# A gate build on VectorE alone, with the dense stage's pools opened before the build: a two-layer hybrid network with product-key experts on one Trainium2 core

## Chip, cores and metric

One core of a Trainium2 chip runs the whole program in one launch. The metric is the device time of one execution in microseconds (us), lower is better.

## What is computed

Two layers over 512 latent and 256 context tokens of width 1024, in float32. Each layer is a normalisation, an input projection, three parallel groups of heads, an output projection, and then a feed-forward part of 16384 experts, of which each token uses 8 x 16. The change lies in this last part alone:

```
s = einsum('nhpd,hpkd->nhpk', (tok @ wq), sub_keys)      # 8 heads x 2 halves x 128 keys
idx, gate = top 16 of the 256 sums of the two top-16 lists, softmax     # per token and head
a = gelu(einsum('nd,nhkd->nhk', x, u_tab[idx])) * gate
out = einsum('nhk,nhkd->nd', a, v_tab[idx])
```

## The kernel before

The program is traced with Python loops that are fully unrolled. The framework puts the instructions of each engine into one fixed order, at compile time, by their place in the program (earlier goes first) and by when its own model of time thinks them ready; on the chip each engine, and the queue of DMA issues of SyncE (SP), runs its list strictly in that order and waits on semaphores. Tiles of a pool with the same tag share its buffers, and a pool that closes leaves its memory to the next one opened on the same side, once its tiles are released.

The expert part (`peer_lat`, L1268) does most latent tokens (512 in layer 0, 384 in layer 1) *densely*: instead of fetching experts, it multiplies all tokens with all 16384 experts in 128 blocks of 128, and a sparse matrix G [token, expert] of gates sets what counts. The rest (256 context tokens in layer 0, the last 128 latent tokens in layer 1) is *gathered*: generators (`gather`, L1208) fetch rows of `peer_uv` (u and v of one expert per partition, 8 KB each) with an indirect DMA issued on GpSimd (L1249) and use them with two VectorE instructions (L1231 dot product, L1223 accumulation). One step of a generator handles two such fetches. The order is:

1. `route` (L1050): scores, top 16, indices and gates.
2. `build_g` (L1308): G is made by products of one-hot matrices. An iteration handles 8 tokens: VectorE compares index halves with an iota (`goa` L1353, `gob` L1354), multiplies by the high half of the gate (`o1`, L1355) and the low half (`o2`, L1359; the trace calls both `go`), 16 small float16 matmuls (128x128) multiply them, ScalarE scales two PSUM banks into `gst` (L1365), and after four iterations SP stores 2 MB to `Gd` in DRAM (L199). 64 iterations in layer 0, 48 in layer 1. Of the `o2`, every third is on VectorE, the others on GpSimd.
3. `dense` (L1396): for each block c: load and split u into high and low float32r parts (`duh` L1377 on ScalarE, `dul` L1378), 24 matmuls for the hidden values (L1383) and a GELU (`dge` L1386); load and split v (L1450, L1451); multiply with G (`dcf`, then `dch`, `dcl`); 24 output matmuls of the block before (helper, L141). One load of G (`dG`, L1444) serves four blocks. Gather steps are spread over the 128 blocks (L1464).

To give TensorE something in route and build, the hidden values of some blocks are made *early* (`early`, L1389): 26 blocks (1, 6, ..., 126) in each layer, stored to DRAM, and loaded again in the dense stage (`Hd`). In them `dul` is computed on GpSimd. `advance` says where in the program a block stands: 8 after the route (L1288), one per five iterations of the build (L1357), the rest after the build (L1297). `steps(STEP_BUILD)` (L1358) puts 0.15 or 0.1 gather steps into each iteration.

Pools: `pe` (u and hidden of the early blocks, left side) closes before the dense stage; `pu`, `pg` (gathered rows, six buffers) open before the build; `gk`, `gw` belong to the build; `dw` holds all tiles of the dense stage and opens on the right side after the build has closed. PSUM changes hands at the same place (`pps.close()`, L1302): 2 banks `sm` for early blocks and 4 `mm` for the build before it, 6 or 7 `o` and 2 or 1 `h` after it.

Of the kernel before, what the change touches and what calls it, by code (L numbers as in the profile page):

```python
# [10 lines left out]
F32R = mybir.dt.float32r  # L11
# [5 lines left out]
OP = mybir.AluOpType  # L17
# [4 lines left out]
P = 128  # L22
D = 1024
# [20 lines left out]
SB = 4  # L44
TB = 32
UVB = 6
STEP_BUILD = (0.15, 0.1)
RH = 2
ROUTE = (0, 0)
TAIL = (8, 8)  # L50
EARLY = (tuple(range(1, 128, 5)), tuple(range(1, 128, 5)))
GSC = 32768.0
ADA_BUFS = 3
ADA_PROJ = 0.7
# [32 lines left out]
class Kern:  # L87
    def __init__(self, ctx, tc, a, dbg=None):
        self.ctx, self.tc, self.nc, self.a = ctx, tc, tc.nc, a
        self.dbg = dbg  # L90
        self.uid = 0
        self.ev = 0
        self.bg = []
        self.bg2, self.owed = None, 0.0
        self.todo = 0
        self.pace = 0.0
        self.clock = 0.0
        self.rate = 0.0
        self.gelu = False
        self.hold = False  # L100

    def pool(self, st, name, bufs=1, space=None, side=None):
        kw = {}
# [1164 lines left out]
    def peer_lat(self, l, jobs, xt, sx, pps):  # L1268
        nc, a = self.nc, self.a
        nd = DENSE[l]  # L1270
        last = SEQ // P - 1
        with ExitStack() as st:
            pk = self.pool(st, "pdk", side="right")
            xh, xl = x = tuple(self.T(pk, [P, KD, SEQ], F32R, tag="x" + t) for t in "hl")
            sr, se, spu = ExitStack(), ExitStack(), ExitStack()
            run(self.norm(l, 1, 0, x, xt, side="right"))
            sx.close()
            pr = self.pool(sr, "pdr", side="left")
            self.gelu = True
            if nd < SEQ:  # L1280
                with ExitStack() as s1:
                    xT = self.T(self.pool(s1, "xT", side="right"), [P, KD, P], tag="xT")
                    ts = slice(last * P, SEQ)
                    nc.vector.tensor_add(xT, xh[:, :, ts].bitcast(F32), xl[:, :, ts].bitcast(F32))
                    xn = self.token_major(pr, xT, 0)
            self.bg2 = self.early(l, self.pool(se, "pe", 2), xh, xl)
            r = self.route(l, 0, x, pr)
            self.advance(TAIL[l])  # L1288
            self.pu = self.pool(spu, "pu", 1, side="right")
            pg = self.pool(spu, "pg", 1, side="right")  # L1290
            self.bg = [self.gather(pg, l, 1, i, *job) for i, job in enumerate(jobs)]
            if nd < SEQ:
                self.bg.append(self.gather(pg, l, 0, last, xn, *r[last]))
            self.todo = len(self.bg) * (HK // 2 + 3)
            with ExitStack() as s1:
                self.build_g(s1, l, r)
            run(self.bg2 or ())  # L1297
            self.bg2 = None
            se.close()
            if nd == SEQ:  # L1300
                sr.close()
            pps.close()  # L1302
            with ExitStack() as s1:
                self.dense(s1, l, xh, xl)
            spu.close()
            sr.close()

    def build_g(self, st, l, r):  # L1308

        nc, a = self.nc, self.a  # L1310
        T = self.T
        nd = DENSE[l]
        pk = self.pool(st, "gk", side="right")
        pw = self.pool(st, "gw", 2, side="right")
        iota = T(pw, [P, P], tag="iotag")
        self.load(iota, a["iota"])
        iota4 = T(pk, [P, P, 4], F16, tag="iota4")
        nc.vector.tensor_copy(iota4, iota[:, :, None].to_broadcast([P, P, 4]))
        e16 = [T(pk, [P, nd], F16, tag=f"e16{j}") for j in range(4)]
        for i in range(-(-nd // P)):  # L1320
            idx, gate = r[i]
            ts = slice(i * P, min((i + 1) * P, nd))
            m = ts.stop - ts.start
            for j in range(3):
                if j == 2:
                    src = gate
                else:
                    ii = T(pw, [P, HK], I32, tag="gii")
                    if j == 0:
                        nc.vector.tensor_scalar(ii, idx, 7, 127, op0=OP.logical_shift_right, op1=OP.bitwise_and)  # L1330
                    else:
                        nc.vector.tensor_scalar(ii, idx, 127, None, op0=OP.bitwise_and)
                    src = T(pw, [P, HK], tag="gif")
                    nc.vector.tensor_copy(src, ii)
                pt = self.ps("tr")
                self.tr(pt[:, :P], src)
                if j < 2:
                    nc.scalar.copy(e16[j][:, ts], pt[:, :m])
                else:

                    sg = T(pw, [P, P], tag="gsg")
                    nc.scalar.activation(sg[:, :m], pt[:, :m], AF.Copy, scale=GSC)
                    nc.scalar.copy(e16[2][:, ts], sg[:, :m])
                    nc.vector.tensor_sub(e16[3][:, ts], sg[:, :m], e16[2][:, ts])
        n = 0
        for tb in range(nd // TB):
            stage = T(pw, [P, P, TB], tag="gst")
            for q in range(TB // 8):
                c0 = tb * TB + q * 8
                bc = lambda e: e[:, c0:c0 + 8].rearrange("p (g t) -> p g t", t=4)[:, :, None, :].to_broadcast([P, 2, P, 4])  # L1350
                it = iota4[:, None].to_broadcast([P, 2, P, 4])
                oa, ob, o1, o2 = (T(pw, [P, 2, P, 4], F16, tag=f"go{x}") for x in "ab12")
                nc.vector.tensor_tensor(oa, bc(e16[0]), it, op=OP.is_equal)  # L1353
                nc.vector.tensor_tensor(ob, bc(e16[1]), it, op=OP.is_equal)  # L1354
                nc.vector.tensor_tensor(o1, oa, bc(e16[2]), op=OP.mult)  # L1355
                n += 1
                self.advance(0.2)  # L1357
                self.steps(STEP_BUILD[l])  # L1358
                (nc.vector if n % 3 == 0 else nc.gpsimd).tensor_tensor(o2, oa, bc(e16[3]), op=OP.mult)  # L1359
                for g in range(2):  # L1360
                    gp = self.ps("mm")
                    for t in range(4):
                        for j, o in enumerate((o1, o2)):
                            self.mm(gp[:, t * P:(t + 1) * P], ob[:, g, :, t], o[:, g, :, t], j == 0, j == 1)
                    nc.scalar.activation(stage[:, :, q * 8 + g * 4:q * 8 + g * 4 + 4].rearrange("p i t -> p t i"),  # L1365
                                         gp.rearrange("p (t i) -> p t i", i=P), AF.Copy, scale=1.0 / GSC)
            self.load(self.Gd[l][:, :, tb, :].rearrange("s j x -> j s x"),
                      stage.rearrange("p (s i) t -> p s (i t)", i=SB))
# [20 lines left out]
    def early(self, l, pool, xh, xl):  # L1389

        for c in EARLY[l]:
            ge = self.hidden(l, c, pool, pool, xh, xl, "sm", self.nc.gpsimd)
            self.load(self.Hd[l, c], ge)
            yield

    def dense(self, st, l, xh, xl):  # L1396
        nc, a = self.nc, self.a
        T = self.T
        nd = DENSE[l]
# [40 lines left out]

        todo, done = self.todo - DEFER[l], 0
        for sb in range(NC // SB):
            G = T(pw, [P, nd // TB, SB, TB], tag="dG")
            self.load(G.rearrange("p b i t -> p b (i t)"), self.Gd[l][sb])  # L1444
            for ci in range(SB):
                c = sb * SB + ci
                v = T(pw, [P, D], tag="dv")
                self.load(v, a["peer_v"][l, c * P:(c + 1) * P, :])
                vh, vl = (T(pw, [P, D], F32R, tag="dv" + x, bufs=2 + rest) for x in "hl")
                nc.scalar.copy(vh, v)  # L1450
                nc.vector.tensor_sub(vl, v, vh.bitcast(F32))  # L1451
                if c in EARLY[l]:
                    ge = T(pw, [P, nd], tag="dge")
                    self.load(ge, self.Hd[l, c])
                else:
                    ge = self.hidden(l, c, pw, pw, xh, xl, "h", nc.vector)
                cf = T(pw, [P, nd], tag="dcf", bufs=1)
                nc.vector.tensor_mul(cf.rearrange("p (b t) -> p b t", t=TB), ge.rearrange("p (b t) -> p b t", t=TB),
                                     G[:, :, ci, :])
# [7 lines left out]
                if prev is not None:  # L1467
                    add(*prev)
                prev = (c, ch, cl, vh, vl)
        gB = T(pw, [P, D], tag="du")  # L1470
        self.load(gB, self.grow[l][1][0:1, :].to_broadcast([P, D]))
        xs = [T(pw, [P, D], tag=t) for t in ("dG", "dv", "dv", "dG")[:NT + rest]]
        for t, x in enumerate(xs):
            self.load(x, self.xsrc(l, 1, 0, t))
        add(*prev)
# [3 lines left out]
        for t, x in enumerate(xs):  # L1479
            for hf in range(2):  # L1480
                hs = slice(hf * 512, (hf + 1) * 512)
                tmp = T(pw, [P, 512], tag="duh")
                nc.vector.tensor_mul(tmp, o[t][hf] if t < NT else o4[:, hf], gB[:, hs])
                nc.vector.tensor_add(x[:, hs], x[:, hs], tmp)
            nc.gpsimd.dma_start(self.xdst(l, 1, 0, t), x)
# [172 lines left out]
```

## Time and profile before

| | |
|---|---|
| time, median of 3 runs (range) | 4478.73 us (4469.4 to 4480.89) |
| the profiled execution: time, span | 4476.18 us, 4474.4 us |
| mean granted TensorE clock | 0.94 |
| busy: TensorE matmul, VectorE, GpSimd, ScalarE | 89%, 73%, 38%, 35% |
| layer 0: build, gap, dense stage | 1012 to 1294 us, to 1317.5 us, to 2607 us |
| layer 1: build, gap, dense stage | 3286 to 3483.6 us, to 3500 us, to the end |

Rows of groups give the line, the engine, the operation, output <- inputs, shapes and xcount, then the busy time, the mean time of one in ns, and the idle time of the engine before them with what ended it. PE is TensorE, PEld its weight loads, DVE VectorE, ACT ScalarE, POOL GpSimd. Matmul ends are modelled: a matmul's own duration overlaps the next one's, so a sum of durations is not time; the busy time of many is.

### The profile page before, as it was taken

To read this page: it belongs to the slowest core of one execution; us is meant where nothing else is said; L and a number is where in the kernel's file an instruction comes from. 1 tells how busy PE (TensorE), PEld (TensorE's weight loads), DVE (VectorE), ACT (ScalarE), POOL (GpSimd) and SP (SyncE) were. 2 spreads that over 40 slices of the span, in tenths; PEclk is the share of its full clock that TensorE was granted. 3 is DMA by queue.
4 is the path that set the end of the run, shared out by engine and by line. 5 is a ranking of instruction groups with operands and counts; after the bars stand their busy time and mean duration, and the time that the engine had idled before them with its cause. 6 is when DMAs were issued, how large, how long until landed. Compare 5 with 4: busy or idle time off the path is not lost. (4 is left out here: it accounts for less than half of the span.)

```text
span 4474.4 us, 57073 instructions
## 1 busy us (share of the span) xinstructions
PE 3992.0 (89%) x20829; PEld 3352.4 (75%) x20829; DVE 3283.9 (73%) x6347; ACT 1571.2 (35%) x2562; POOL 1705.1 (38%) x1363
## 2 busy tenths in 40 slices
PE   7889878877869999999999969888868899999998
PEld 4568657666658888777888859677667799999998
DVE  2444686589978888788888755674889577777775
ACT  2332243325543333223323233433246333333332
POOL 2133354785633333233333133345876222222220
PEclk8899889988879999999999989989978899999999
DMA  7663221317779889888889634123257788788875
GB/s 264 226 208 108 60 71 62 112 61 221 227 250 352 332 333 335 322 319 324 338 334 343 247 114 119 50 81 100 65 164 216 265 307 303 294 311 301 301 300 168
DMA packets 429346, 996.46 MB, mean 223 GB/s; under 512 B 31448, under 2 KB 264280, under 8 KB 375816
## 3 DMA queue, kind: packets, MB, share of 16 engines
q1 hardware_dynamic: 372760, 586.46, 38.3%
q0 software_dynamic: 56304, 406.35, 24.4%
q8 instruction: 164, 2.69, 0.2%
q14 instruction: 118, 0.97, 0.1%
HBM read 909.97 MB, written 81.17 MB: 222 GB/s over the span
## 5 line engine op out<-in xcount | busy, mean ns | idle before, releaser
L1249 POOL DMA_INDIRECT uv<-in_peer_uv_dram,ridx x384 | 633.3, 1649 | 1558.2 <-DVE eacc L1223 1506.8
L141 PE MATMUL o<-dvh,dch 128*128 128x512 f32 x1792 | 702.0, 392 | 3.5 <-DVE do L1425 3.5
L141 PE MATMUL o<-dvl,dch 128*128 128x512 f32 x1792 | 701.3, 391 | 0.0
L141 PE MATMUL o<-dvh,dcl 128*128 128x512 f32 x1792 | 697.2, 389 | 0.0
L1383 PE MATMUL h<-xh,duh 128*128 128x512 f32 (+1 forms) x1632 | 602.9, 369 | 47.5 <-ACT duh L1377 39.9
L1383 PE MATMUL h<-xh,dul 128*128 128x512 f32 (+1 forms) x1632 | 604.8, 371 | 0.4 <-DVE dul L1378 0.3
L1383 PE MATMUL h<-xl,duh 128*128 128x512 f32 (+1 forms) x1632 | 602.2, 369 | 0.0
L1223 DVE SCALAR_TENSOR_TENSOR eacc<-uv,egf,eacc 128x1024 f32<-128x1024 f32 x381 | 492.4, 1293 | 0.0
L1231 DVE SCALAR_TENSOR_TENSOR uv<-uv,xn 128x1024 f32<-128x1024 f32 x384 | 470.3, 1225 | 0.0
L1377 ACT CAST duh<-du 128x1024 fp32r<-128x1024 f32 x256 | 268.7, 1050 | 535.4 <-PE h L1383 455.6
L1378 DVE TENSOR_TENSOR dul<-du,duh 128x1024 fp32r<-128x1024 f32 x204 | 249.5, 1224 | 261.9 <-ACT duh L1377 225.6
L141 PEld LDWEIGHTS o<-dvh,dch 128*128 128x128 f32 x1792 | 336.3, 188 | 78.1 <-DVE do L1425 7.2
L141 PEld LDWEIGHTS o<-dvh,dcl 128*128 128x128 f32 x1792 | 336.5, 188 | 73.6 <-DVE dcl L1462 0.3
L141 PEld LDWEIGHTS o<-dvl,dch 128*128 128x128 f32 x1792 | 336.3, 188 | 66.6
L1450 ACT CAST dvh<-dv 128x1024 fp32r<-128x1024 f32 x256 | 263.1, 1051 | 350.1 <-PE o L141 298.0
L1451 DVE TENSOR_TENSOR dvl<-dv,dvh 128x1024 fp32r<-128x1024 f32 x256 | 308.8, 1221 | 101.5 <-ACT dvh L1450 82.1
L1383 PEld LDWEIGHTS h<-xh,duh 128*128 128x128 f32 x1632 | 309.1, 189 | 90.2 <-ACT duh L1377 40.5
L1383 PEld LDWEIGHTS h<-xl,duh 128*128 128x128 f32 x1632 | 309.0, 189 | 42.1
L1383 PEld LDWEIGHTS h<-xh,dul 128*128 128x128 f32 x1632 | 308.6, 189 | 39.1 <-DVE dul L1378 1.9
L141 PE MATMUL mm<-go,gob 128*128 128x128 f16 x1792 | 238.1, 297 | 94.0 <-DVE go L1355 79.0
L141 PEld LDWEIGHTS <-gob 128*128 128x128 f16 x1792 | 194.8, 120 | 141.4 <-DVE go L1355 100.6
L1365 ACT ACTIVATE gst<-mm 128x512 f32<-128x512 f32 x224 | 226.3, 1120 | 166.3 <-PE mm L141 153.6
(352 smaller groups left out, 8027.9 us busy)
## 6 DMA issues: line engine op xcount, KB each, us to landing
du<-in_peer_ut_dram SPq DMA_DIRECT2D x256, 512.0 KB
dv<-in_peer_v_dram SPq DMA_DIRECT2D x256, 512.0 KB
Gd<-gst SPq DMA_DIRECT2D x28, 2048.0 KB
wa<-in_w_ada_dram SPq DMA_DIRECT2D x24, 2048.0 KB
w<-in_w_in_dram SPq DMA_DIRECT2D x78, 512.0 KB
dG<-Gd SPq DMA_DIRECT2D x32, 1024.0 KB
w<-in_peer_wq_dram SPq DMA_DIRECT2D x48, 512.0 KB
dG<-Gd SPq DMA_DIRECT2D x32, 768.0 KB
```

Source lines behind the costliest of these rows:

```text
L141: self.nc.tensor.matmul(out, lhsT=lhsT, rhs=rhs, start=start, stop=stop)
L1223: nc.vector.scalar_tensor_tensor(acc, t[:, D:], w, acc, op0=OP.mult, op1=OP.add)
L1231: nc.vector.scalar_tensor_tensor(t[:, :D], t[:, :D], 1.0, xn, op0=OP.mult, op1=OP.mult, accum_out=dots[:, k:k + 1])
L1249: nc.gpsimd.indirect_dma_start(t, None, a["peer_uv"], bass.IndirectOffsetOnAxis(ap=idx[:, k:k + 1], axis=0))
L1365: nc.scalar.activation(stage[:, :, q * 8 + g * 4:q * 8 + g * 4 + 4].rearrange("p i t -> p t i"), gp.rearrange("p (t i) -> p t i", i=P), AF ...
L1377: nc.scalar.copy(uh, u)
L1378: eng.tensor_sub(ul, u, uh.bitcast(F32))
L1383: nc.tensor.matmul(hp[:, :nd], lhsT=lt[:, k], rhs=rt[:, k, :nd], start=n == 0, stop=n == 3 * KD - 1)
L1450: nc.scalar.copy(vh, v)
L1451: nc.vector.tensor_sub(vl, v, vh.bitcast(F32))
```

## The change

`o2` is always on VectorE; no gather step stands in the build; the early blocks that are emitted inside the build loop take `dul` on VectorE (those ahead of and behind the loop stay on GpSimd); 25 blocks are early (3, 8, ..., 123). `pe` stays open through the dense stage, whose u and hidden tiles come from it. A new pool `pv` for v, its halves and G opens before the build, `pu` and `pg` after it. In block 0 the load of G is emitted behind the load of u. The tiles of the final addition come from other tags.

```
-STEP_BUILD = (0.15, 0.1)
-EARLY = (tuple(range(1, 128, 5)), tuple(range(1, 128, 5)))
+EARLY = (tuple(range(3, 128, 5)), tuple(range(3, 128, 5)))
...
-            self.bg2 = self.early(l, self.pool(se, "pe", 2), xh, xl)
+            pe = self.pool(se, "pe", 2)
+            self.bg2 = self.early(l, pe, xh, xl)
             r = self.route(l, 0, x, pr)
             self.advance(TAIL[l])
+            pv = self.pool(spu, "pv", 2, side="right")
+            self.building = True
+            with ExitStack() as s1:
+                self.build_g(s1, l, r)
+            self.building = False
+            run(self.bg2 or ())
+            self.bg2 = None
             self.pu = self.pool(spu, "pu", 1, side="right")
...
-            with ExitStack() as s1:
-                self.build_g(s1, l, r)
-            run(self.bg2 or ())
-            self.bg2 = None
-            se.close()
-            if nd == SEQ:
-                sr.close()
             pps.close()
             with ExitStack() as s1:
-                self.dense(s1, l, xh, xl)
+                self.dense(s1, l, xh, xl, pe, pv)
             spu.close()
+            se.close()
             sr.close()
...
+                nc.vector.tensor_tensor(o2, oa, bc(e16[3]), op=OP.mult)
                 self.advance(0.2)
-                self.steps(STEP_BUILD[l])
-                (nc.vector if n % 3 == 0 else nc.gpsimd).tensor_tensor(o2, oa, bc(e16[3]), op=OP.mult)
...
-            ge = self.hidden(l, c, pool, pool, xh, xl, "sm", self.nc.gpsimd)
+            ge = self.hidden(l, c, pool, pool, xh, xl, "sm", self.nc.vector if self.building else self.nc.gpsimd)
...
-            G = T(pw, [P, nd // TB, SB, TB], tag="dG")
-            self.load(G.rearrange("p b i t -> p b (i t)"), self.Gd[l][sb])
+            G = T(pv, [P, nd // TB, SB, TB], tag="dG")
+            if sb:
+                self.load(G.rearrange("p b i t -> p b (i t)"), self.Gd[l][sb])
...
-                    ge = self.hidden(l, c, pw, pw, xh, xl, "h", nc.vector)
+                    ge = self.hidden(l, c, pe, pe, xh, xl, "h", nc.vector)
+                if c == 0:
+                    self.load(G.rearrange("p b i t -> p b (i t)"), self.Gd[l][0])
...
-        gB = T(pw, [P, D], tag="du")
+        gB = T(pv, [P, D], tag="dv")
...
-        xs = [T(pw, [P, D], tag=t) for t in ("dG", "dv", "dv", "dG")[:NT + rest]]
+        xs = [T(p, [P, D], tag=t) for p, t in ((pv, "dG"), (pv, "dG"), (pv, "dv"), (pe, "du"))[:NT + rest]]
...
-                tmp = T(pw, [P, 512], tag="duh")
+                tmp = T(pe, [P, 512], tag="dge")
```

In `dense` the tiles `dv`, `dvh`, `dvl` move from `pw` to `pv` and the early blocks' `dge` from `pw` to `pe` in the same way.

## Rows read from the trace of the kernel before

**Rows 1.** The page: busy time of the engines, and one group of instructions
```profile
PE 3992.0 (89%) x20829; PEld 3352.4 (75%) x20829; DVE 3283.9 (73%) x6347; ACT 1571.2 (35%) x2562; POOL 1705.1 (38%) x1363
...
L1378 DVE TENSOR_TENSOR dul<-du,duh 128x1024 fp32r<-128x1024 f32 x204 | 249.5, 1224 | 261.9 <-ACT duh L1377 225.6
```

**Rows 2.** Busy time by stretch: both builds, the gaps behind them, dense stages
```profile
core 0: us, PE busy (x) PEld busy (x) DVE busy (x) ACT busy (x) POOL busy (x), PEclk, DMA share, GB/s
...
1012.00:1294.00 282.00, 223.89 (x1387) 180.15 (x1385) 268.32 (x278) 151.69 (x178) 166.41 (x76) 0.87 0.70 223
1294.00:1317.50 23.50, 0.04 (x1) 0.04 (x1) 3.90 (x8) 3.33 (x5) 2.71 (x2) 0.50 0.87 301
1317.50:2400.00 1082.50, 1071.36 (x4602) 867.65 (x4603) 932.13 (x1255) 326.55 (x491) 351.17 (x212) 0.99 0.88 331
...
3286.00:3483.60 197.60, 157.77 (x1062) 139.20 (x1060) 187.22 (x185) 113.22 (x132) 121.07 (x53) 0.85 0.67 209
3483.60:3500.00 16.40, 0.01 (x1) 0.02 (x1) 1.07 (x1) 2.58 (x3) 0.00 (x0) 0.58 0.94 309
3500.00:4400.00 900.00, 899.65 (x4446) 811.66 (x4447) 668.10 (x885) 331.88 (x493) 197.89 (x118) 1.00 0.79 296
```

**Rows 3.** Groups of instructions in the build of layer 0
```profile
L141 PE MATMUL mm<-go,gob 128*128 128x128 f16 x1024 | 136.2, 297 | 55.4 <-DVE go L1355 48.4 <-POOL go L1359 5.5 <-DVE go L1359 0.4
...
L1359 POOL TENSOR_TENSOR go<-goa,e 128x1024 f16<-128x1024 f16 x43 | 99.5, 2318 | 85.8 <-DVE goa L1353 59.9 <-PE mm L141 21.9 <-DVE e L1344 2.9
L1355 DVE TENSOR_TENSOR go<-goa,e 128x1024 f16<-128x1024 f16 x64 | 98.2, 1534 | 0.0
L1353 DVE TENSOR_TENSOR goa<-e,iota 128x1024 f16<-128x1024 f16 x64 | 62.3, 981 | 0.1
...
L1378 POOL TENSOR_TENSOR dul<-du,duh 128x1024 fp32r<-128x1024 f32 x14 | 39.3, 2809 | 5.3 <-ACT duh L1377 3.6 <-issue 1.7
...
L1223 DVE SCALAR_TENSOR_TENSOR eacc<-uv,egf,eacc 128x1024 f32<-128x1024 f32 x14 | 22.7, 1625 | 0.0
L1231 DVE SCALAR_TENSOR_TENSOR uv<-uv,xn 128x1024 f32<-128x1024 f32 x17 | 20.5, 1212 | 0.0
L1359 DVE TENSOR_TENSOR go<-goa,e 128x1024 f16<-128x1024 f16 x21 | 14.3, 680 | 0.0
```

**Rows 4.** VectorE in order of time in the build of layer 0 (start, us)
```profile
1055.16 2.38 DVE L1355 TENSOR_TENSOR go<-goa,e 128x1024 f16<-128x1024 f16 x1
1057.46 0.68 DVE L1353 TENSOR_TENSOR goa<-e,iota 128x1024 f16<-128x1024 f16 x1
...
1059.87 0.68 DVE L1353 TENSOR_TENSOR goa<-e,iota 128x1024 f16<-128x1024 f16 x1
```

**Rows 5.** Matmuls of line 1383 alone, by stretch (busy, count; clock, DMA)
```profile
1012.00:1294.00 282.00, 110.81 (x355) 69.10 (x353) 0.87 0.70 223
...
3286.00:3483.60 197.60, 74.27 (x288) 55.45 (x287) 0.85 0.67 209
...
3500.00:4400.00 900.00, 425.75 (x2304) 411.93 (x2305) 1.00 0.79 296
```

**Rows 6.** SP's queue, then TensorE, at the end of layer 0's build
```profile
1295.06 0.37 SPq L199 DMA_DIRECT2D Gd<-gst  x1
1309.03 0.33 SPq L199 DMA_DIRECT2D dG<-Gd  x1
...
1309.88 0.42 SPq L199 DMA_DIRECT2D du<-in_peer_ut_dram  x1
...
1317.46 0.80 PE L1383 MATMUL h<-xh,duh 128*128 128x512 f32 x1 [23.53 <-ACT duh L1377]
```

**Rows 7.** SP's queue at the end of layer 1's build
```profile
3482.57 0.37 SPq L199 DMA_DIRECT2D Gd<-gst  x1
...
3491.41 0.32 SPq L199 DMA_DIRECT2D dG<-Gd  x1
```

**Rows 8.** Waits of SP's queue, layer 0's build: us, times, longest
```profile
SPq L199 <- ACT gst L1365: 130.6, 18, 12.4
```

More of the change, by code (lines that the diff above doesn't have):

```diff
@@ L1285, in peer_lat @@
                     xn = self.token_major(pr, xT, 0)
-            self.bg2 = self.early(l, self.pool(se, "pe", 2), xh, xl)
+            pe = self.pool(se, "pe", 2)
+            self.bg2 = self.early(l, pe, xh, xl)
             r = self.route(l, 0, x, pr)
             self.advance(TAIL[l])
+            pv = self.pool(spu, "pv", 2, side="right")
+            self.building = True
+            with ExitStack() as s1:
+                self.build_g(s1, l, r)
+            self.building = False
+            run(self.bg2 or ())
+            self.bg2 = None
             self.pu = self.pool(spu, "pu", 1, side="right")
@@ L1344, in build_g @@
                     nc.vector.tensor_sub(e16[3][:, ts], sg[:, :m], e16[2][:, ts])
-        n = 0
         for tb in range(nd // TB):
@@ L1355, in build_g @@
                 nc.vector.tensor_tensor(o1, oa, bc(e16[2]), op=OP.mult)
-                n += 1
+                nc.vector.tensor_tensor(o2, oa, bc(e16[3]), op=OP.mult)
                 self.advance(0.2)
-                self.steps(STEP_BUILD[l])
-                (nc.vector if n % 3 == 0 else nc.gpsimd).tensor_tensor(o2, oa, bc(e16[3]), op=OP.mult)
                 for g in range(2):
@@ L1391, in early, with dense @@
         for c in EARLY[l]:
-            ge = self.hidden(l, c, pool, pool, xh, xl, "sm", self.nc.gpsimd)
+            ge = self.hidden(l, c, pool, pool, xh, xl, "sm", self.nc.vector if self.building else self.nc.gpsimd)
             self.load(self.Hd[l, c], ge)
             yield
-    def dense(self, st, l, xh, xl):
+    def dense(self, st, l, xh, xl, pe, pv):
         nc, a = self.nc, self.a
@@ L1442, in dense @@
         for sb in range(NC // SB):
-            G = T(pw, [P, nd // TB, SB, TB], tag="dG")
-            self.load(G.rearrange("p b i t -> p b (i t)"), self.Gd[l][sb])
+            G = T(pv, [P, nd // TB, SB, TB], tag="dG")
+            if sb:
+                self.load(G.rearrange("p b i t -> p b (i t)"), self.Gd[l][sb])
             for ci in range(SB):
                 c = sb * SB + ci
-                v = T(pw, [P, D], tag="dv")
+                v = T(pv, [P, D], tag="dv")
                 self.load(v, a["peer_v"][l, c * P:(c + 1) * P, :])
-                vh, vl = (T(pw, [P, D], F32R, tag="dv" + x, bufs=2 + rest) for x in "hl")
+                vh, vl = (T(pv, [P, D], F32R, tag="dv" + x, bufs=2 + rest) for x in "hl")
                 nc.scalar.copy(vh, v)
@@ L1452, in dense @@
                 if c in EARLY[l]:
-                    ge = T(pw, [P, nd], tag="dge")
+                    ge = T(pe, [P, nd], tag="dge")
                     self.load(ge, self.Hd[l, c])
                 else:
-                    ge = self.hidden(l, c, pw, pw, xh, xl, "h", nc.vector)
+                    ge = self.hidden(l, c, pe, pe, xh, xl, "h", nc.vector)
+                if c == 0:
+                    self.load(G.rearrange("p b i t -> p b (i t)"), self.Gd[l][0])
                 cf = T(pw, [P, nd], tag="dcf", bufs=1)
```

## The prediction, made before the change was run

> **What bounds the kernel now.** The page comes first: TensorE's matmuls are busy 89% of the span, VectorE 73% [rows 1]. Such a share is a mean over stages, so the next view is the busy time by stretch [rows 2]. In the two dense stages TensorE is busy 1071.36 of 1082.5 us and 899.65 of 900, at clock 0.99 and 1.00: they can lose, but hardly win. In the two builds it is busy 223.89 of 282 and 157.77 of 197.6 us, at 0.87 and 0.85, while VectorE is busy 268.32 (95%) and 187.22 (95%). Behind each build stands a gap, 23.5 and 16.4 us, in which no compute engine works. What can be won lies in 282 + 23.5 + 197.6 + 16.4 = 519.5 us; the rest of the span is taken as it is.
>
> The groups of the build show why VectorE is full [rows 3]. In the idle time ahead of the build's matmuls 48.4 of 55.4 us end with `o1`. The same kind of product, same shapes, takes 680 ns as `o2` and on average 1534 as `o1`; `goa` takes 981. In order of time [rows 4] an `o1` has 2.38 us where a GpSimd product runs, and five instructions, 1057.46 to 1059.87, start 0.60 us apart where none does. VectorE and GpSimd hold each other up here: a product given to GpSimd (2318 ns) lengthens the one VectorE does meanwhile by about 1.7 us, more than the 0.6 it spares.
>
> **Part 1, `o2` on VectorE, no gather steps, early `dul` on VectorE.** An iteration costs VectorE four products at 0.60, 2.41 us by the starts in [rows 4]. Layer 0: 64 x 2.41 = 154, twelve `dul` in the loop (advance: 8 + 0.2 x 64) at 1.22 [rows 1] = 15, the five blocks behind the loop still on GpSimd at 1.7 of hindrance = 9, some 6 of set-up (an estimate): 184 us. Layer 1: 116 + ten `dul` 12 + seven blocks 12 = 140 and a few. The gather takes 20.5 + 22.7 = 43 us out of the first build [rows 3].
>
> TensorE then sets the pace. Layer 0: the 1024 small matmuls have 136.2 us [rows 3]; 355 hidden matmuls were in the build [rows 5], one block of 24 goes, and at 1071.36 / 4602 = 0.233 us [rows 2] 331 cost 77: 213 us. Layer 1: 768 at the same 0.133 = 102, plus 264 at 425.75 / 2304 = 0.185 [rows 5] = 49: 151. ScalarE (151.69 and 113.22 us busy) stays below. No build has run TensorE-bound, so the excess over this floor lies between 0 and 15% (it is 26% and 24% of TensorE's busy time now, with VectorE in the way; in a dense stage 1%). I take 5%, nearer the dense stage, because the lists are again fixed by a model that sees TensorE with slack: 224 and 159 us. **Gain 58 and 38.6 us** (37 to 69, 24 to 47).
>
> The Trainium skill, Perfetto Trace Analysis, "Optimizing Scalar/DVE Operations", says that offloading to GpSimd may make sense when VectorE is saturated, which speaks against taking work back at 95%, and adds that between these two it might not help, as they share a port. By its first half the builds would not get shorter (the third rival); [rows 4] are the measurement of its second half, and the sum goes by them.
>
> **Part 2, the pools opened ahead.** Now G's last store goes out at 1295.06, its load can go at 1309.03, and u and v stand behind it in SP's list although they don't need it; the first matmul starts at 1317.46 [rows 6]. In layer 1 store and load are 3482.57 and 3491.41 [rows 7]. With `pe` and `pv` open, v and u of blocks 0 and 1 can be there before the build ends, and u of block 2 as soon as a buffer is free; blocks 0 to 2 are not early, so TensorE has three hidden blocks that need no G: 3 x 24 x 0.233 = 16.8 us, and 13.3 in layer 1. Of the gaps 6.7 and 3.1 us stay, and some 2 us in layer 1 until the PSUM banks change hands: I take 6 and 5. **Gain 17.5 and 11.4 us**; bounds nothing and the whole gap. Late next is G itself: its wait now stands behind one u and v, and the loads queued behind it (v, u of later blocks) wait for it in SP's list. `pu` opens in memory that the build gives up, so six row fetches of 1 MiB start just then, on DMA engines that were 0.87 busy in the gap; that is inside the bounds.
>
> **Part 3, small ones.** One block less is early: its 24 matmuls, counted out of the builds above, are in the dense stages, 5.6 and 4.4 us **lost**, and its `dul` now costs VectorE there; one store and load of its hidden values less, at nothing. The moved gather steps (some 9 and 4) add 43 us to a VectorE that is idle 1082.5 - 932 = 150 us in the stretch of layer 0's dense stage shown, beside a bound TensorE: hidden, but its DMA rises from 0.88 to about 0.92 busy (20 MB more on some 425). I take 4 us **lost**, from 0 to 12; without the cover all 43 would show. The tiles of the last addition come from other tags with the same number of buffers and their loads stand behind two free slots: nothing, or one load (the 8.4 us from 1309.03 to 1317.46, [rows 6]) if a slot is late. `pe` and the route's results held longer: the next layer starts from the dense stage's output anyway, nothing.
>
> **Sum**: 58 + 38.6 + 17.5 + 11.4 - 5.6 - 4.4 - 4 = 111.5 us. The profiled execution took 4476.2, so 4364.7; the median of the runs is 2.5 above it: **4367 us**.
>
> **Rivals.**
> *The gaps stay.* If v and u of block 1 stay behind G's wait in SP's list, or PSUM passes on late, hardly more than nothing of the 28.9 us is won: 82.6 gained, 4396. For it: SP's list has had that order. Against it: the buffers now exist before the build ends. 0.18.
> *TensorE's list is poor.* With 15% over the floor (245 and 174), bare gaps and 12 us lost in the dense stages, 37 + 24 - 10 - 12 = 39 to 60 us are gained: about 4427. For it: lists fixed by a model; 0.13.
> *VectorE is not relieved* (the change doesn't do what it says, and what the skill's first half would give): durations stay, and VectorE takes over 43 + 32 products at 0.68 and 22 `dul` at 1.22, less the gathers: 268 - 43 + 29 + 15 = 269 in layer 0 (nothing won) and 187 + 22 + 12 - 21 = 200, 13 more, in layer 1. With the gaps and part 3 the sum is +2: 4477. Against it: [rows 4]. 0.06.
> *VectorE stands behind `dul`* (slower). On GpSimd a subtraction that waited for its u held up little; on VectorE all products of the build are queued behind it, and TensorE behind those. SP waits up to 12.4 us for a `gst` [rows 8], with u queued behind it. If each of the 22 `dul` waited that long: 273 us, 162 more than all gains, 4640. It decides from a wait of about (111 + 40 of VectorE's slack) / 22 = 7 us each. Against it: before, 14 of them waited 3.6 us together for `duh` [rows 3]. 0.05.
>
> **Numbers.** The forecast has 0.58. With the best bounds (69 + 47 + 40 - 10 = 146) the time is 4333; the poor list ends at 4440. The range 4330 to 4425 leaves out the slower rival, the third one and part of the second. A measurement of this kernel can tell 0.3%, 13 us, from no change. Faster: 0.58 + 0.18 + 0.13 = 0.89; same 0.06; slower 0.05.
>
> **What would show it.** Right: `o1` and `goa` near 680 ns on average; builds of about 224 and 159 us with TensorE above 90% busy, clock near 1; hidden matmuls within a few us of the last small one, before G lands; dense stages within some 10 us. Wrong: `o1` still above 1 us; VectorE idle in the build behind `duh`; gaps above 15 us; a dense stage with DMA at 0.95 or more and TensorE waiting for u.

## The result, and the profile after

The changed kernel takes 4374.32 us (median of 4 runs, 4370.12 to 4378.36) against 4479.81 for the kernel before on the same chip: a ratio of 0.9768, 95% interval 0.9747 to 0.9788. The prediction was 4367. The profiled execution has a span of 4368.4 us, 106.0 less than before.

The page of the kernel after: busy time by engine, then groups [rows 1, 3].

```profile
PE 3969.8 (91%) x20829; PEld 3338.2 (76%) x20829; DVE 3179.7 (73%) x6446; ACT 1570.0 (36%) x2562; POOL 1467.7 (34%) x1264
...
L1377 DVE TENSOR_TENSOR dul<-du,duh 128x1024 fp32r<-128x1024 f32 x228 | 278.6, 1222 | 303.3 <-ACT duh L1376 287.5
...
L141 PE MATMUL mm<-go,gob 128*128 128x128 f16 x1792 | 232.9, 296 | 8.7 <-DVE go L1357 5.8
```

The last line holds the first part of the result: over both builds the small matmuls now wait 8.7 us, where layer 0's alone waited 55.4. (Lines behind L1346 moved up by one.) The groups of layer 0's build say why [rows 3]:

```profile
L141 PE MATMUL mm<-go,gob 128*128 128x128 f16 x1015 | 133.8, 296 | 4.6 <-DVE go L1357 4.2 <-ACT gst L1364 0.2
...
L1356 DVE TENSOR_TENSOR go<-goa,e 128x1024 f16<-128x1024 f16 x64 | 43.8, 684 | 0.0
L1357 DVE TENSOR_TENSOR go<-goa,e 128x1024 f16<-128x1024 f16 x64 | 43.7, 683 | 0.0
L1354 DVE TENSOR_TENSOR goa<-e,iota 128x1024 f16<-128x1024 f16 x64 | 43.3, 684 | 0.0
```

`o1` (L1356) takes 684 ns instead of 1534, `goa` 684 instead of 981: within 4 ns of what `o2` took on VectorE before (680). All 64 `o2` have come to VectorE, and VectorE is busy 173 us where it was 268.

Busy time by stretch: layer 0's build, what follows it up to the first dense hidden matmul, its dense stage, then the same of layer 1 [rows 2].

```profile
1002.10:1197.00 194.90, 190.26 (x1287) 159.41 (x1286) 173.24 (x277) 148.20 (x165) 4.91 (x2) 0.94 0.74 212
1197.00:1231.30 34.30, 25.28 (x117) 20.79 (x115) 3.79 (x3) 10.71 (x13) 13.10 (x9) 0.93 0.96 344
1231.30:2400.00 1168.70, 1166.59 (x5030) 945.71 (x5031) 1050.40 (x1427) 354.87 (x543) 410.15 (x246) 1.00 0.91 349
...
3185.60:3339.00 153.40, 139.71 (x1004) 128.60 (x1003) 129.05 (x207) 111.27 (x127) 11.24 (x2) 0.90 0.70 205
3339.00:3387.60 48.60, 33.81 (x162) 31.33 (x160) 1.60 (x2) 11.93 (x16) 19.68 (x12) 0.82 0.85 308
3387.60:4300.00 912.40, 912.37 (x4501) 813.88 (x4502) 682.91 (x907) 333.82 (x499) 204.21 (x122) 1.00 0.79 298
```

Both builds became much shorter (282 to 194.9 us, 197.6 to 153.4). But what lies behind them grew, from 23.5 to 34.3 and from 16.4 to 48.6 us, and its nature changed: TensorE now works there. What it works on is in the same view of the hidden matmuls alone (L1382; a block is 24 of them). The stretches are route, build, and what follows, of each layer:

```profile
770.00:1002.10 232.10, 63.43 (x232) 47.37 (x232) 0.85 0.26 81
1002.10:1197.00 194.90, 72.98 (x264) 48.23 (x262) 0.94 0.74 212
1197.00:1231.30 34.30, 24.28 (x106) 19.85 (x106) 0.93 0.96 344
2800.00:3185.60 385.60, 46.87 (x211) 41.92 (x211) 0.86 0.23 73
3185.60:3339.00 153.40, 49.66 (x231) 42.20 (x230) 0.90 0.70 205
3339.00:3387.60 48.60, 33.81 (x162) 31.33 (x160) 0.82 0.85 308
```

In layer 0, 232 matmuls (9.7 blocks) ran ahead of the build, 264 in it, and 106 (over four blocks) are left behind it; in layer 1 8.8, 9.6 and 6.8 blocks. These left-over *early* blocks, not blocks 0 to 2 of the dense stage, now stand behind the builds, and TensorE idles 9 us after them in layer 0 and 15 us among them in layer 1. In the kernel before, 271 and 338 matmuls (11.3 and 14.1 blocks) ran ahead of the builds, by the same view of its two routes, and the rest, 355 and 288, in them [rows 5]:

```profile
780.00:1012.40 232.40, 74.61 (x271) 55.81 (x272) 0.89 0.28 86
...
2800.00:3286.70 486.70, 70.82 (x338) 65.09 (x338) 0.91 0.24 75
```

Cut at the first `goa`, the first dense hidden matmul and the last output matmul of each layer (before, that of layer 0 is at 2611.6 us, behind the 2607 of the table above), the 106.0 us are:

| stretch | before | after | difference |
|---|---|---|---|
| up to layer 0's build | 1012.4 | 1002.1 | -10.3 |
| layer 0, build and what follows | 305.1 | 229.2 | -75.9 |
| layer 0, dense stage | 1294.1 | 1287.5 | -6.6 |
| up to layer 1's build | 675.1 | 666.8 | -8.3 |
| layer 1, build and what follows | 213.3 | 202.0 | -11.3 |
| layer 1, dense stage to the end | 974.4 | 980.8 | +6.4 |

Layer 0 won what was forecast (-75.5). Layer 1 won 11 us where 50 were forecast, so the runs had two things to find: whether the products on VectorE are the cause of the shorter builds, and where layer 1's gain went.

### The profile page after: what moved, and what is told of

Same layout as the page of the kernel before. It is cut to its first block, busy times and chain, and to the rows that moved or that the text cites. A ratio compares the mean times of both kernels' runs of the same rounds, so it can differ in the third digit from the quotient of the medians.

```text
span 4368.4 us, 56981 instructions
## 1 busy us (share of the span) xinstructions
PE 3969.8 (91%) x20829; PEld 3338.2 (76%) x20829; DVE 3179.7 (73%) x6446; ACT 1570.0 (36%) x2562; POOL 1467.7 (34%) x1264
## 4 chain that ended last, share of the span: by engine, by line
PE 58%; DVE 5%; issue 3%; DMA 3%; POOL 3%; ACT 1%; SPq 0%; POOLq 0%; ACTq 0%; DVEq 0%
PE o L141 27%; PE h L1382 22%; PE mm L141 6%; PE sm L1382 2%; DMA du<-in_peer_ut_dram 2%; POOL roh L1174 1%; PE tr L196 0%; POOL dul L1377 0%; PE sm L141 0%; DMA w<-in_w_in_dram 0%; DVE req L1172 0%; POOL wl L321 0%; DVE go L1356 0%; DVE go L1357 0%; DVE gob L1355 0%
## 5 line engine op out<-in xcount | busy, mean ns | idle before, releaser
L141 PE MATMUL o<-dvl,dch 128*128 128x512 f32 x1792 | 711.1, 397 | 0.0
L141 PE MATMUL o<-dvh,dcl 128*128 128x512 f32 x1792 | 707.1, 395 | 0.0
L1382 PE MATMUL h<-xh,duh 128*128 128x512 f32 (+1 forms) x1648 | 600.5, 364 | 12.5 <-ACT dge L1385 12.5
L1382 PE MATMUL h<-xl,duh 128*128 128x512 f32 (+1 forms) x1648 | 599.8, 364 | 0.0
L1382 PE MATMUL h<-xh,dul 128*128 128x512 f32 (+1 forms) x1648 | 598.5, 363 | 0.0
L1377 DVE TENSOR_TENSOR dul<-du,duh 128x1024 fp32r<-128x1024 f32 x228 | 278.6, 1222 | 303.3 <-ACT duh L1376 287.5
L1382 PEld LDWEIGHTS h<-xh,duh 128*128 128x128 f32 x1648 | 309.9, 188 | 53.8 <-ACT dge L1385 14.1
L1382 PEld LDWEIGHTS h<-xl,duh 128*128 128x128 f32 x1648 | 310.0, 188 | 37.2
L1382 PEld LDWEIGHTS h<-xh,dul 128*128 128x128 f32 x1648 | 310.0, 188 | 34.2
L1463 ACT CAST dch<-dcf 128x512 fp32r<-128x512 f32 (+1 forms) x256 | 145.2, 567 | 316.8 <-DVE dcf L1460 302.3
L1364 ACT ACTIVATE gst<-mm 128x512 f32<-128x512 f32 x224 | 223.2, 1145 | 22.4 <-PE mm L141 17.5
```

What stands on the lines that cost most here:

```text
L141: self.nc.tensor.matmul(out, lhsT=lhsT, rhs=rhs, start=start, stop=stop)
L1377: eng.tensor_sub(ul, u, uh.bitcast(F32))
L1382: nc.tensor.matmul(hp[:, :nd], lhsT=lt[:, k], rhs=rt[:, k, :nd], start=n == 0, stop=n == 3 * KD - 1)
L1463: m1 = nc.scalar.copy(ch, cf)
```

## The experiments

All of them compute the whole result. Each time stands beside runs of the kernel before on the same chip (4474 to 4478 us).

**1. `o2` alone.** The kernel before with

```
-                (nc.vector if n % 3 == 0 else nc.gpsimd).tensor_tensor(o2, oa, bc(e16[3]), op=OP.mult)
+                nc.vector.tensor_tensor(o2, oa, bc(e16[3]), op=OP.mult)
```

> The kernel before, with every o2 on VectorE; gather steps, the early dul on GpSimd and all pools stay. Theory A (GpSimd's products beside VectorE's are what filled VectorE): o1 falls from 1534 ns to under 900 on average, the builds to about 240 and 168 us (VectorE 154 + 51 of gather + 24 hindered by 14 dul + 6, and alike in layer 1), gaps of 23 and 16 us stay; about 4408 us, 0.984. Theory B (the build got shorter because the gather left it, who makes o2 matters little): o1 stays above 1.3 us, VectorE has 75 x 0.68 = 51 us more; about 4520 us, slower.

4399.35 us, 0.9838 (0.982 to 0.9855): theory A. Two groups of its layer 0 build, then both builds:

```profile
L1359 DVE TENSOR_TENSOR go<-goa,e 128x1024 f16<-128x1024 f16 x64 | 48.1, 752 | 0.0
L1355 DVE TENSOR_TENSOR go<-goa,e 128x1024 f16<-128x1024 f16 x64 | 47.9, 749 | 0.0
```
```profile
1010.50:1245.00 234.50, 210.05 (x1370) 167.41 (x1369) 225.69 (x324) 153.68 (x177) 74.14 (x35) 0.90 0.84 270
...
3236.10:3405.00 168.90, 149.99 (x1059) 131.30 (x1059) 152.47 (x215) 114.83 (x133) 42.40 (x21) 0.89 0.78 245
```

Giving VectorE 43 more products made its `o1` twice as fast and its busy time 42.6 us *less* (225.69 for 268.32). That is the contention, shown by one edit; and 75 us come from this one line. The row that [rows 4] lack is GpSimd's product beside the `o1` of 1055.16:

```profile
1055.08 1.91 POOL L1359 TENSOR_TENSOR go<-goa,e 128x1024 f16<-128x1024 f16 x1 [1.59 <-DVE goa L1353]
```

**2. Everything but the products.** The kernel after, with two `o2` of three and every early `dul` on GpSimd.

```
-                nc.vector.tensor_tensor(o2, oa, bc(e16[3]), op=OP.mult)
+                (nc.gpsimd if (tb * (TB // 8) + q) % 3 != 2 else nc.vector).tensor_tensor(o2, oa, bc(e16[3]), op=OP.mult)
...
-            ge = self.hidden(..., self.nc.vector if self.building else self.nc.gpsimd)
+            ge = self.hidden(..., self.nc.gpsimd)
```

> The kernel after, with two thirds of o2 and all early dul back on GpSimd: what stays are the pools, the order of G's load, the gather moved behind the build and 25 early blocks. Theory A: builds of about 235 and 178 us (VectorE's 268 and 187 less 51 and 19 of gather, with the idle time of before), gaps mostly filled; about 4398 us, 24 behind the kernel after; o1 stays above 1.3 us. Theory B: as the kernel after, 4374 within 10 us. Theory C (the pools do nearly all): the same.

4399.19 us, 0.9836 (0.9816 to 0.9857), as expected. `o1` is back at the slow price, with no gather step in the build, so these steps were not what slowed it:

```profile
L1357 POOL TENSOR_TENSOR go<-goa,e 128x1024 f16<-128x1024 f16 x43 | 105.2, 2452 | 89.4 <-DVE goa L1354 70.7 <-PE sm L1382 10.6 <-DVE e L1346 6.7
L1356 DVE TENSOR_TENSOR go<-goa,e 128x1024 f16<-128x1024 f16 x64 | 102.7, 1605 | 0.0
```

**3. The gather steps alone**, taken out of the kernel before's builds (`STEP_BUILD = (0.0, 0.0)`).

> The kernel before, with no gather step in the build and nothing else changed. Theory: VectorE sets the build's pace, so all of the gather's 51 and 19 us come off it: builds of about 232 and 180 us, 4 us given back in the dense stages, about 4412 us. Rival (the gather stands in VectorE's idle time beside GpSimd's products): 4465 or more.

4442.69 us, 0.993 (0.9913 to 0.9946): 35 us, between the two expectations. The forecast of the theory took all of the steps' 70 us as gained in the builds and 4 as lost behind them. Builds and gaps gave 55 (260.2 for 305.1 us, 202.8 for 213.3), with `o1` still at 1589 ns, and layer 0's dense stage, which took the steps, became 16 us longer (1310.2 for 1294.1).

**4. No new pools.** The kernel before with all `o2` and the `dul` inside the loop on VectorE and `STEP_BUILD` 0.

```
-STEP_BUILD = (0.15, 0.1)
+STEP_BUILD = (0.0, 0.0)
...
+            self.building = True
             with ExitStack() as s1:
                 self.build_g(s1, l, r)
+            self.building = False
...
-                (nc.vector if n % 3 == 0 else nc.gpsimd).tensor_tensor(o2, oa, bc(e16[3]), op=OP.mult)
+                nc.vector.tensor_tensor(o2, oa, bc(e16[3]), op=OP.mult)
...
-            ge = self.hidden(l, c, pool, pool, xh, xl, "sm", self.nc.gpsimd)
+            ge = self.hidden(l, c, pool, pool, xh, xl, "sm", self.nc.vector if self.building else self.nc.gpsimd)
```

> The kernel before, with o2 and the in-loop dul on VectorE and no gather step in the build, but pools, early blocks 1, 6, ... and G's load as before. Theory A: builds as in the kernel after (about 195 and 153 us), behind them gaps of some 20 and 15 us without a matmul, unless early blocks left over stand there: 4374 + 25 = about 4400 us. Theory C (the pools do nearly all of the 105 us): above 4440 us.

4396.29 us, 0.983 (0.9808 to 0.9852). As a number this is what was expected. But `o2` (75 us) and the gather steps (35) alone give 110, and this kernel, which has both, gives only 78. Either the two gains don't add, or the one thing that it has besides, `dul` on VectorE, costs something. For the second speaks that 232 and 211 hidden matmuls run ahead of its builds, as in the kernel after, though pools and early blocks are the old ones; where every early `dul` is on GpSimd (the kernel before, experiments 1 to 3) they are 271 to 281 and 338 to 344.

**5. `dul` back on GpSimd**, all else as in the kernel after.

```
-            ge = self.hidden(..., self.nc.vector if self.building else self.nc.gpsimd)
+            ge = self.hidden(..., self.nc.gpsimd)
```

> The kernel after, with the early dul of the build loop on GpSimd again. Theory A: VectorE is hindered by some 1.7 us for each of 22 subtractions but has slack beside TensorE (184 against 213 us, 140 against 151), and blocks are pulled into the route again (11 and 14 ahead of the build in place of 9.7 and 8.8): 4374 within 13 us. Rival D (the place of dul decides, either because GpSimd's subtraction hinders VectorE's products or because VectorE stood behind it): 20 us or more away, slower in the first case, faster in the second.

4326.27 us, 0.9671 (0.9654 to 0.9687): 48 us *faster* than the kernel after, and the fastest of all that ran. (The two ran on different chips; by their ratios to the kernel before on the same chip it is 43.) So theory A is out, the faster case of rival D has come, and this part of the change, taken for a gain of nothing or little, costs 43 to 48 us. The sum fits: `o2` 75, gather 35, and the pools 40 (experiment 2's 75 less those 35) are 150, and this kernel, which has these three and no `dul` on VectorE, gains 148. That they add up so exactly is no proof of each: the pools alone, and `o2` with the gather steps but without `dul`, were not run. The hidden matmuls alone, in the same six stretches:

```profile
770.00:1009.80 239.80, 75.55 (x271) 57.01 (x272) 0.87 0.27 86
1009.80:1214.00 204.20, 104.27 (x330) 56.74 (x329) 0.98 0.71 208
1214.00:1235.30 21.30, 18.12 (x67) 13.95 (x67) 0.85 0.98 337
2800.00:3186.30 386.30, 72.34 (x343) 66.54 (x343) 0.89 0.26 83
3186.30:3332.00 145.70, 61.89 (x259) 43.42 (x258) 0.93 0.74 217
3332.00:3350.70 18.70, 15.79 (x66) 15.03 (x66) 0.78 1.00 346
```

Again 271 and 343 matmuls run ahead of the builds, as in the kernel before, and none of an early block behind them: the 67 and 66 there are blocks 0 to 2 of the dense stage. The first of them follows the build's last small matmul after 1.27 us of idle TensorE (TensorE in order of time):

```profile
1215.76 0.79 PE L1382 MATMUL h<-xh,duh 128*128 128x512 f32 x1 [1.27 <-ACT gst L1364]
```

From the first `goa` to this point layer 1 now takes 145.7 us instead of 202.0, layer 0 206.0 instead of 229.2; the two routes with the more blocks in them take 7.7 and 14.0 more.

**6. Is it only the number of blocks ahead?** The kernel after, `dul` in the loop still on VectorE, with more blocks emitted right behind the route.

```
-TAIL = (8, 8)
+TAIL = (11, 14)
```

> The kernel after (in-loop dul on VectorE), but 11 and 14 early blocks are emitted right behind the route, with dul on GpSimd, in place of 8 and 8: as many as run ahead of the build where all dul are on GpSimd. Theory E (what dul on VectorE cost is the blocks that no longer fill TensorE's idle time in the route and queue up behind the build): 11 and 14 blocks ahead of the build again, no tail of early blocks behind it, about 4335 us (4322 to 4348). Theory F (VectorE's subtractions in the build itself cost it): 4360 to 4380, although the blocks stand ahead.

4348.16 us, 0.9712 (0.9696 to 0.9729), at the far edge of what E said: 272 and 341 matmuls ahead of the builds, as in experiment 5, and somewhat over half of its advantage. Layer 0's build is then as good as there (209.3 to the first dense matmul, 206.0 there); layer 1's is not (163.6 against 145.7).

**7, 8, 9. Three smaller edits**: the kernel after with `dul` of the blocks behind the loop on VectorE too (7); the same on top of experiment 6 (8); and experiment 6 with `dul` on GpSimd in layer 1 alone (9).

```
# 7 and 8
-            self.building = False
             run(self.bg2 or ())
             self.bg2 = None
+            self.building = False
# 9
-            self.building = True
+            self.building = l == 0
```

> The kernel after, with dul on VectorE also for the early blocks behind the loop, where VectorE is idle. Theory E: each of the 5 and 7 chains of u, cast, dul, 24 matmuls in the tail is 1.2 us shorter, if u is there: 4360 to 4374. Rival (late u loads set the tails, DMA 0.96 and 0.85 busy there): 4374 within 6 us.

> The kernel with more blocks placed ahead of the build (4348 us), with the dul of the blocks behind the loop on VectorE too. Theory S, one GpSimd subtraction of 10.49 us beside back-to-back VectorE products, with TensorE 8.1 us behind it, is what layer 1's build still loses: L1's build 160.8 becomes about 150, total 4336 (4330 to 4342). Theory U, the loss is u landing late (ScalarE waited 15.9 us for it in eight waits), because the subtractions inside the loop stand behind products in VectorE's list and free u late: nothing changes, 4348 (4343 to 4354).

> The same kernel of 4348 us, with dul inside the loop on GpSimd in layer 1 alone. If the 22 us that still separate it from the kernel with every early dul on GpSimd (4326) sit in layer 1's build: 4330 (4324 to 4336), L1 build 146 with TensorE idle 4 us. If the place of dul is worth as much in layer 0: half of it, about 4337 and more, with L0's build left at 203.

Number 7: 4363.58 us, 0.974 (0.9724 to 0.9756), some 10 us better than the kernel after and in the range of theory E, though its interval overlaps that of the kernel after. What it gains is seen in layer 1: from the first `goa` to the first dense matmul 189.1 us instead of 202.0. In the kernel after TensorE waits there 9.9 us for subtractions on GpSimd, in number 7 for none; its waits for `duh` fell too, from 13.1 to 5.1 us. Most of the 9.9 us is one row of the kernel after, and not, as E had it, 1.2 us in each block. GpSimd, VectorE and TensorE in order of time near the end of layer 1's build:

```profile
3317.26 10.90 POOL L1377 TENSOR_TENSOR dul<-du,duh 128x1024 fp32r<-128x1024 f32 x1 [142.38 <-PE mm L141]
```
```profile
3323.01 0.69 DVE L1357 TENSOR_TENSOR go<-goa,e 128x1024 f16<-128x1024 f16 x1
3323.61 2.36 DVE L1451 TENSOR_TENSOR dvl<-dv,dvh 128x1024 fp32r<-128x1024 f32 x2
```
```profile
3328.22 0.69 PE L1382 MATMUL sm<-xh,dul 128*128 128x384 f32 x1 [8.45 <-POOL dul L1377]
```

The subtraction stands for 10.90 us while VectorE runs product after product, and it ends 2.2 us after VectorE's row does; TensorE sits idle 8.45 us behind it. Number 8: 4342.4 us, 0.97 (0.9682 to 0.9717). Number 9: 4336.66 us, 0.969 (0.9673 to 0.9706). Both lie between their expectations, and the intervals of 6, 8 and 9 overlap one another, so the totals decide little; the stretches say more, though each is of one execution. Layer 1's build in 6, 8 and 9:

```profile
3191.20:3352.00 160.80, 142.76 (x1028) 132.67 (x1027) 131.85 (x210) 112.27 (x128) 10.49 (x1) 0.92 0.69 205
```
```profile
3194.30:3347.10 152.80, 142.66 (x1034) 132.70 (x1032) 133.29 (x212) 113.68 (x130) 0.00 (x0) 0.92 0.72 213
```
```profile
3191.80:3339.40 147.60, 143.54 (x1029) 125.64 (x1027) 135.91 (x200) 115.70 (x127) 22.65 (x9) 0.92 0.73 213
```

The same 143 us of TensorE work stand in 160.8, 152.8 and 147.6 us. The first step is the one starved GpSimd subtraction (10.49 us here), the second is `dul` of the loop standing in VectorE's list. In 6 and 8 ScalarE still waited 15.9 and 16.5 us for loads of u, in eight waits each; in 9 there is no such wait. The other 11 us between 9 and 5 (spans 4332.9 and 4322.0) lie mostly in the dense stages (4.8 and 3.5); their cause stays open.

**10. The order of the first loads.** The kernel after with the load of G again ahead of v and u in block 0.

```
-            if sb:
-                self.load(G.rearrange("p b i t -> p b (i t)"), self.Gd[l][sb])
+            self.load(G.rearrange("p b i t -> p b (i t)"), self.Gd[l][sb])
...
-                if c == 0:
-                    self.load(G.rearrange("p b i t -> p b (i t)"), self.Gd[l][0])
```

> The kernel after, with the load of G in block 0 ahead of the loads of v and u again. Theory: five early blocks left over stand between the build and block 0, G (issued at 1209.75) is there long before its first use (1242.28): 4374 within 8 us. Rival (the order of G's load is what fills the gap): the gap opens, 4385 to 4400.

4369.8 us, 0.9764 (0.9748 to 0.9781): no difference. With left-over blocks still in TensorE's list, G's place in SP's list does not decide; on top of experiment 5, where none are left over, it was not tried.

**11. More early blocks**, on experiment 5.

```
-TAIL = (8, 8)
-EARLY = (tuple(range(3, 128, 5)), tuple(range(3, 128, 5)))
+TAIL = (14, 18)
+EARLY = (tuple(range(3, 127, 4)), tuple(range(3, 127, 4)))
```

> The kernel with every early dul on GpSimd (4326 us), with 31 instead of 25 early blocks (3, 7, ..., 123) and 14 and 18 instead of 8 of them placed right behind the route. If the six more run in the route, where TensorE is busy 63 of 232 us and the DMA engines 0.26, the dense stages have six blocks less: 6 x 24 x (0.233 + 0.185) = 60 us gained, 4266 (4255 to 4285). Rival: they crowd into the build or behind it, or lengthen the route, and what the dense stage saves is paid there: 4315 to 4335.

4369.86 us, 0.9763 (0.9747 to 0.978): 44 us *slower* than experiment 5, worse than even the rival said. The expectation misread a row: 63 us is the hidden matmuls' share of the route, while TensorE's whole busy time there is 179.7 of 232.1, at a granted clock of 0.85. The route is no free room: the six blocks lengthened layer 0's route by 24.6 us, the builds by 13.7 and 24.5. Layer 1's dense stage paid back 27.5, layer 0's nothing, it took 14.4 more. There TensorE, which experiment 5 keeps busy 200.00 of 200 us, now waits (mainly for ScalarE's `dge`, 26.9 us in the stage):

```profile
1300.00:1500.00 200.00, 189.32 (x802) 151.72 (x801) 171.39 (x236) 56.49 (x88) 73.63 (x42) 0.98 0.86 333
```

## Why the prediction was right, and where not

**The contention: right, and the main term.** That a product on GpSimd lengthens its neighbour on VectorE by more than it spares was read from five instructions [rows 4]; experiments 1 and 2 show it from both sides, and `o1`, `o2` and `goa` stand at 683 to 684 ns, 4 from the 680 forecast. The third rival is out. For these products in this build, the first half of what the Trainium skill says (Perfetto Trace Analysis, "Optimizing Scalar/DVE Operations"), that offloading from a saturated VectorE may make sense, does not hold; its second half, that it might not help between these two, is what the runs show, more strongly: taking work back helped by 75 us.

**The builds: right in mechanism, too cautious in layer 0.** Forecast 224 and 159 us, measured 194.9 and 153.4. The allowance of 5% over TensorE's floor was wrong in layer 0: 136.2 us of small matmuls [rows 3] and the 264 hidden ones that stood there at 0.233 make 198, so nothing was lost (TensorE 98% busy). In layer 1, 102 + 231 x 0.185 = 145, and 153.4 is 6% over, which is the one wait of 8.45 us shown under number 7. (Of the excess before, the forecast's 24% is 25%: 197.6 for 157.77.) The larger part of the miss in layer 0 is the next point.

**The failing step: "331 hidden matmuls in the build", "the gaps go from 23.5 to 6 and from 16.4 to 5".** Part 1 took the matmuls counted in the builds before, less one block, and thereby held fixed how many blocks run ahead of the build. Putting `dul` on VectorE changed that. Fewer blocks ran in the routes (9.7 and 8.8 for 11.3 and 14.1), and over four and nearly seven came to stand behind the builds. Experiment 5 undoes `dul` alone, and the count ahead and the empty space behind come back, with 330 and 259 hidden matmuls in the builds where 331 and 264 were forecast; experiment 6 restores the count alone, and brings over half of the gain. The rest of the gain is open but for the single subtraction of experiment 7 and the loads of u. Why the compile-time list is so is argued only: a subtraction among the build's products in VectorE's list holds its block's matmuls there, while on GpSimd nothing holds them back. So "from the gap 17.5 and 11.4 us gained" came true in experiment 5, not in this kernel. There blocks 0 to 2 did follow the build at once (1.27 us of idle TensorE in each layer), just as Part 2 described.

**The tails.** What follows the builds is not TensorE-bound either. The waits of the kernel after, first behind layer 0's build, then in layer 1 from the first `goa` on (us, times, longest):

```profile
ACT duh L1376 <- DMA du<-in_peer_ut_dram: 15.7, 2, 11.5
```
```profile
ACT duh L1376 <- DMA du<-in_peer_ut_dram: 22.2, 9, 9.4
...
PE sm L1382 <- ACT duh L1376: 13.1, 5, 7.2
```

In layer 0 the four left-over blocks themselves ran without a hole, up to 1222.28 us. Then TensorE stood for 9.07 us, all of its idle time there, though u of block 0 had been cast and split by 1219.02. What released it is the GELU of the last left-over block, which reads a PSUM bank that the dense stage takes over (`pps.close()`); and that GELU stood in ScalarE's list behind the cast of block 1's u (ScalarE, then TensorE, in order of time):

```profile
1229.76 1.04 ACT L1376 CAST duh<-du 128x1024 fp32r<-128x1024 f32 x1 [11.52 <-DMA du<-in_peer_ut_dram]
1230.71 0.59 ACT L1385 ACTIVATE dge<-sm 128x512 f32<-128x512 f32 x1
```
```profile
1231.35 0.80 PE L1382 MATMUL h<-xh,duh 128*128 128x512 f32 x1 [9.07 <-ACT dge L1385]
```

So a late load that TensorE did not need yet held back PSUM that it did need. The bound that Part 2 set aside, row fetches that start just when the build ends, is the likely reason for the late load: the DMA engines are 0.96 and 0.85 busy behind the builds, moving 344 and 308 GB/s, while u is late. No run moves the fetches, so this is argued only.

**What offset it.** Part 3 forecast 14 us lost (5.6, 4.4, and 4 for the moved gather). The dense stages together won 0.2, in spite of one block more each: layer 0's TensorE idles 2.1 us of the stretch shown where it idled 11.1 [rows 2]. The gather was hidden as argued, with VectorE at 90% and the DMA engines at 0.91; but with the old pools it was not: in experiments 3 and 4 layer 0's dense stage takes 1310.2 and 1311.2 us for 1294.1, more than the 12 us that Part 3 allowed, and why the new pools change this stays open. And the routes, taken as unchanged, became 10.3 and 8.3 us shorter, since they held fewer blocks (layer 1's route was no shorter than before in experiment 4, 675.5 us with as few blocks, so not all of the 8.3 need be this). So layer 1's build and what follows it gave 38.7 us less than forecast, and routes and dense stages 32.8 more. That the total was right to 7 us is in part luck: two errors were the two sides of one, as blocks that left the route came back behind the build, and the dense stages' 14 us are an error of its own.

**The rivals.** "The gaps stay" came near in figures (82.9 us now lie behind the builds, 39.9 before), and in layer 0 its second condition came true, PSUM that passes on late (9.07 us). The rest is not its mechanism: left-over blocks and late u fill the time, and experiment 10 shows that here the order of G, v and u was nothing. "TensorE's list is poor" had the right object in the wrong stage: the list was good in the builds and poor in which stage held which block. "VectorE stands behind `dul`" was set aside on the right grounds, VectorE hardly stood (in the two builds it waited 19.9 and 11.3 us for TensorE, and not once for `duh`); but `dul` did its harm in another way, by its place, not by a stall, and that rival should have been worked out for the list as well as for the wait.

## What to carry to other kernels

When two engines contend, measure one instruction with and without its neighbour: here one such pair of rows was worth 75 us. When a change moves an instruction to another engine, ask not only what it costs there but in which list it stands from now on, and which work that was filling an idle stage is held back with it; count the filler by stage (matmuls of one line by stretch) before and after. Test each part of a bundle by itself: three parts here gained 148 us together, and the fourth took 43 to 48 back. The version without it, at 4326 us, beats both kernels.

## What the runs showed of the hardware that was not expected

The contention works both ways. A float16 product on VectorE takes 2.38 us beside a product on GpSimd [rows 4] and 0.68 alone; a subtraction on GpSimd, on average 2.81 us in layer 0's build before [rows 3], took 10.90 and 10.49 us where it started while VectorE ran its products back to back. The Trainium skill, SBUF — State Buffer, "Who interferes with whom", says that a VectorE instruction with two inputs in SBUF contends with a GpSimd one that reads SBUF, and that issue order decides which of them waits. The pair of [rows 4] agrees: GpSimd's product started at 1055.08, and the `o1` that started at 1055.16 was the long one. The subtraction of 10.90 us goes beyond it: it started while one VectorE product ran, and ended only after eleven more VectorE instructions that started later than it did; that of 10.49 us in experiment 6 ended after ten such.
